# The modulation filler of the scans: loads of 2048 columns into one buffer in place of 512 into four

## The chip, the cores and the metric

The kernel runs on one core of one Trainium2 chip. The time is the device time of one execution in microseconds (us), the median of several runs. TensorE multiplies; VectorE (DVE), ScalarE (ACT) and GpSimd (POOL) work element by element; SyncE (SP) issues nearly all loads from DRAM.

## The reference, cut to what matters

Two blocks in a row work on 512 latent tokens and 256 context tokens of 1024 channels. The first block has two layers. Each layer's modulation is a product of a short vector with a large matrix, and it shifts, scales and gates everything else in the layer:

```python
silu_c, silu_cc = jax.nn.silu(c), jax.nn.silu(c_ctx)
for l in range(DEPTH):                                   # two layers
    mod_x = (silu_c @ ada_w[l] + ada_b[l])[:, None, :]   # ada_w[l]: 1024 x 6144
    mod_c = silu_cc @ ada_w[l] + ada_b[l]
    ...
    yc, s_f, s_b = rwkv_scans(prep_c, s_zero, s_zero, emit=not last)
    yx, _, _ = rwkv_scans(prep_x, s_f, s_b, emit=True)   # a recurrence over the tokens, both directions
    ...
```

The second block has a modulation of the same size (`w_ada`), attention and a mixture of experts. So there are three modulation matrices of 1024 x 6144, 24 MB each in float32. Each is read once and multiplied with two vectors only (latents and context): there is much to load and little to compute.

## The kernel before, in words

**The modulation.** `ada` (lines 365 to 390) works on groups of 2048 columns; three groups make a matrix, so there are nine. For each of the eight blocks of 128 rows (`k`) it loads pieces of `ada_w` columns (line 373, on SP's queue) into a buffer `wraw` from `raw()` (line 297), and multiplies each 512 columns (line 376): the stationary operand is `cs`, 128 x 32 with the two vectors in its first two columns, the moving operand 128 x 512 in float32. The four 512-column parts of a group go to four column groups of TensorE's array (`tile_position=(0, 32 * q)`) and to four sets of 32 partitions of one PSUM bank, which sums over the eight `k`. A profile shows each such matmul as two records. Afterwards ScalarE copies the bank (line 379) into a buffer `BF`, four transposes (line 382) turn the columns onto the partitions, and VectorE adds the bias.

**Where it runs.** The first group is done before the first layer. The other eight are filler in the scans: `scans` (line 1166) treats four head pairs a layer, and after each it emits `filler(hp)`, which is one group of 2048 columns. Four fall in layer 0's scan (about 365 to 830 us), four in layer 1's (about 1760 to 2215 us).

**The scan around it.** For each head pair `scan_in` prepares the operands (loads of `kr` and of `upr`), `scan_inv` inverts 32 x 32 blocks on VectorE (31 steps of two operations), `scan_x` and `scan_pre` make per-chunk matrices by many small products, loading `UV` on SP's queue, and `scan_run` is the recurrence itself: twelve chunks, at each a few 64 x 64 products on TensorE (lines 910 and 916) and one addition on VectorE that the next chunk's products need. A depthwise convolution (`conv_diag`, tile `cvp`) is spread between them. `BF` has one buffer: the filler's copy comes after the transposes (line 813) of its own head pair, and those of the next pair come after the filler's.

**What sets the order.** The program is built with `schedule_with_timeline_sim=True`: a planner places the instructions of each engine by priority and by its own estimate of the times, and every engine then runs its list strictly in order. Each head pair's filler is emitted with `high_priority(offset=1000)`, so it is placed as soon as its operands are there by that estimate, ahead of the scan's own work.

**The buffers.** `open_r` (line 2166) opens the pools of the scans. There `K.ada_w = 512` and `K.nw = 4`: each load is 128 x 512 (256 KB), and four buffers of 2 KB a partition rotate. A load waits for the matmul that last read its buffer. In the other stages `ada_w` is 1024; the first group, before layer 0, isn't touched.

Of the kernel before, what the change touches and what calls it, by code (L numbers as in the profile page):

```python
# [8 lines left out]
F32 = mybir.dt.float32  # L9
# [15 lines left out]
# ---------------------------------------------------------------- host layout  # L25
class Vecs:
    """Per-channel vectors side by side, channel on the partition."""
# [19 lines left out]
def pack_m(w):  # L47
    """[K, M] -> [M/128, 128, K/128 * 128]: the k-tiles of one column block side by side."""
    k, m = w.shape
    return np.ascontiguousarray(  # L50
        w.reshape(k // 128, 128, m // 128, 128).transpose(2, 1, 0, 3).reshape(m // 128, 128, -1))


def host(I):
# [26 lines left out]
    for l in range(2):  # L81
# [8 lines left out]
        up = np.stack([I["decay_up"][l], I["iclr_up"][l]], 0)               # [2, dir, 64, 512]  # L90
# [6 lines left out]
    qa = w[:, :512].reshape(1024, 2, 4, 64).transpose(0, 2, 1, 3).reshape(1024, 512)   # heads (j, 4 + j) side by side  # L97
# [63 lines left out]
def consts():  # L161
    """Depend on shapes alone."""
# [20 lines left out]
# ---------------------------------------------------------------- the kernel  # L183
# [4 lines left out]
class Stat:  # L188
    """sums of squares over the channels, a column per 128 tokens, from tiles as they come"""
# [24 lines left out]
class Kern:  # L214
    def __init__(self, tc, A, pvat, out, dbg=None):
        self.tw, self.narrow = NT, False
        self.tc, self.nc, self.A, self.at, self.out = tc, tc.nc, A, pvat, out
        self.dbg_out = dbg or {}
        self.V, self.S, self.G, self.T = tc.nc.vector, tc.nc.scalar, tc.nc.gpsimd, tc.nc.tensor
        self.moe_ps, self.queue, self.spare, self.wpre = False, None, [], []  # L220
        self.ada_w = 1024
        self.th = ""               # the strand of work that emits: buffers are handed out in order within each
        self.phm, self.ppm, self.psh = {}, {}, {}     # pools of a strand of its own

    # -- small helpers
# [39 lines left out]
    def rsqrt(self, t, n, name):  # L265
        """t[128, n] > 0 -> 1/sqrt(t), by bits and three Newton steps."""
# [15 lines left out]
    def pin(self, ins):  # L282
        """behind what its engine was given before"""
        return self.tc.keep_in_program_order(ins)
# [11 lines left out]
    # -- weights  # L296
# [18 lines left out]
    def dense(self, src, act, segs, done, kts=8, m=128):  # L315
        """out[m, tok] = w^T act in three passes of float32r; done(i, seg, psum)."""
# [14 lines left out]
    def flush(self, g, mid=None):  # L331
        """the products put off: the first g side by side, a term of each in turn; mid: emitted after their weights;
        what it returns: a step of it per term, done before the last"""
# [20 lines left out]
    # -- adaLN: columns of silu(c) @ w + b, both streams  # L354
# [10 lines left out]
    def ada(self, w, cs, bname, mod, groups, pth=None):  # L365
        """mod[128, 48, 2] += for the groups of 2048 columns."""
        for g in groups:
# [15 lines left out]
            # column q*128 + 32 j + s of tp: block 4 j + q of the group, stream s  # L383
# [8 lines left out]
    # -- rms norm and modulation, channel-major  # L392
    def modcols(self, mod, gname, sh, sc, name):
        """a = g (1 + sc), b = sh for both streams: [128, 8, 2]."""
# [5 lines left out]
    def normstat(self, tiles, segs, name):  # L400
        """1 / rms, on all partitions"""
# [18 lines left out]
    def spread(self, r, segs, name):  # L420
        """a column per 128 tokens as rows on all partitions"""
# [10 lines left out]
    def normmod(self, tiles, segs, a, b, name, streams=None, full=False, dst=None, bcs=None, ahead=False):  # L432
        """hi/lo of rms(x) a + b (full: itself, in dst where given)."""
# [43 lines left out]
    def normmod2(self, tiles, ms, g, a, b):  # L477
        """hi/lo of rms(xb) a + b with xb = rms(x) g, over the latents; then xb in x's place.
        rms(xb)'s mean square is that of x g over the mean square of x; ms: both."""
# [35 lines left out]
    # -- group norm over the 64-channel groups of a tile, tokens at the offsets of segs  # L515
    def gn_center(self, t, segs, name, pin=False):
        """t -= group mean (in place)."""
# [7 lines left out]
    def grp_rstd(self, sq, segs, scale, eps, name, floor=None, rb=None):  # L525
        """psum per seg: rsqrt(sum over the tile's two 64-channel groups * scale + eps)."""
# [23 lines left out]
    # -- token shift of width 3  # L550
# [13 lines left out]
    def wi_tile(self, l, mt, segs, name, out=None):  # L564
        """one column block of the RWKV part of u, shifted. mt counts blocks of 128 after the conv part.
        Where the product is put off, what shifts it."""
# [20 lines left out]
    # -- the scan of one head pair, both directions. Per chunk of 64 tokens:  # L587
    #    A, B (alpha with beta, kappa), D, E (rho with beta, kappa), X = (1 + A)^-1,
    #    U = -X (alpha S + B V), y = rho S + D U + E V, S' = f (S + beta U + kappa V);
    #    with W = X alpha and U0 = -X B V that is S' = M S + c, y = R S + y0 where  # L590
    #    M = f (1 - beta W), c = f (beta U0 + kappa V), R = rho - D W, y0 = D U0 + E V
    def units(self, d, q):
        """first chunk of the direction's batch q"""
        return (8, 0, 4)[q] if d == 0 else (8, 4, 0)[q]
# [5 lines left out]
    def scan_in(self, l, hp, kvs, kt=None, rt=None, kk=None):  # L600
# [9 lines left out]
        off = (self.ph if hp % 2 else ph).tile([128, 24, 32], F32, name="off", bufs=1)      # rows 0-31, 64-95: the block beside the diagonal  # L610
# [21 lines left out]
        for d in range(2):  # L632
# [15 lines left out]
            V.tensor_scalar(thw, thw, -0.5 * DEC, -0.5 * DEC, op0=ALU.mult, op1=ALU.add)   # log decay  # L648
# [28 lines left out]
            # kappa = Eb k (1 + (a - 1) ka), beta = Eb kk a, a = (1 + tha) / 2  # L677
# [11 lines left out]
            # A, for the reverse direction with alpha's token on the partition; its diagonal 32 x 32 blocks go to  # L689
            # lane 8 b + 4 s + i of quadrant (direction, half)  # L690
# [19 lines left out]
    def scan_inv(self, inv=None):  # L710
# [3 lines left out]
        # inverses of the 32 x 32 blocks, one block to a partition  # L714
# [19 lines left out]
    def scan_x(self, off, G1, G2):  # L734
        V, S, G, T = self.V, self.S, self.G, self.T
        # X transposed: diagonal blocks, and -(T2 A21 T1)^T (forward), -(T1 A12 T2)^T (reverse)
# [34 lines left out]
    def scan_pre(self, l, hp, H):  # L771
        """per chunk M and R (over alpha and rho), c and y0"""
# [8 lines left out]
        def early(q, d):  # L781
# [9 lines left out]
            # the two heads on two halves of the rows, side by side  # L791
# [16 lines left out]
            # f beta and f kappa with the token on the partition  # L808
# [10 lines left out]
            # f on the diagonal in alpha's place  # L819
# [69 lines left out]
    def scan_run(self, l, hp, H):  # L889
        """the recurrence over chunks, both directions in step"""  # L890
# [4 lines left out]
        for q in range(3):  # L895
            full = l == 0 or q > 0
            ub = [self.units(d, q) for d in range(2)]
            # the half of the batch with the smaller chunk numbers first
# [30 lines left out]
    def scan_out(self, l, hp, y, kvs, segs, out=None):  # L929
        """group norm, bonus and gate, in place; the last pair's into out"""  # L930
# [31 lines left out]
    def token_terms(self, l, hp, kt, vt, rt, kvs, segs):  # L962
        """normed removal key, bonus of the current token and gate, to DRAM"""
# [4 lines left out]
        # v with the token on the partition  # L968
# [38 lines left out]
    def conv_z(self, l, ci, segs):  # L1007
        """value * sigmoid(gate) (twice), zero-padded: x at 15, ctx at 557."""
# [26 lines left out]
    def conv_taps(self, l, ci, z, segs, pool):  # L1035
        """the depthwise convolution"""
# [20 lines left out]
    def conv_norm(self, l, ci, tiles, segs, mixd):  # L1057
        """twice the silu of the group norm"""
# [21 lines left out]
    def project(self, l, kvs, mixd, zd, lw):  # L1080
        """w_in and the token shift"""
# [9 lines left out]
        # high and low parts over each other: [hi; lo] of w, [lo; hi] of a  # L1091
# [41 lines left out]
    def conv_diag(self, l, ci, zd, segs, steps):  # L1133
        """the depthwise convolution as products with diagonals, in steps"""
# [76 lines left out]
    def mixer_out(self, l, kvs, mixd, mod, spill):  # L1211
        """x + gt1 (mix @ w_out)"""
# [53 lines left out]
    def ffn(self, l, xt, r2, a2, b2, mod):  # L1266
        """x + gt2 (swiglu), in place; the hidden columns in three parts."""
# [56 lines left out]
    # ------------------------------------------------------------ second block  # L1324
# [4 lines left out]
    def rope(self, t, out, name):  # L1329
        """t [128, 512] of the latents -> out"""  # L1330
# [8 lines left out]
    def head_norm(self, t, segs, g):  # L1339
        """rms over the 64 channels of each head, in place."""  # L1340
# [7 lines left out]
    def ctx_ahead(self, mod):  # L1348
        """the second block's normed context"""
# [8 lines left out]
    def qkv(self, xt, ms, mod):  # L1358
        """x (after the first block's norm), queries, keys and token-major values."""
# [25 lines left out]
        def piped(jobs):  # L1385
            """two products ahead of what follows one"""
# [21 lines left out]
        def lat(i):  # L1408
            def first():
# [4 lines left out]
                self.dense(self.A["wqkv"][i], hx, xs, done)    # 0-3 qa, 4 ka, 5-8 qb, 9-12 kb  # L1414
# [22 lines left out]
    def lambda_col(self):  # L1437
        """[128, 1]: minus lambda"""
# [17 lines left out]
    def split_q(self, q, first=False):  # L1456
        """times -1/8, per head, high parts on its own partitions and low parts on the others"""
# [10 lines left out]
    def split_k(self, k, first=False):  # L1468
        """per head, high parts on both halves of the partitions; low parts"""
# [10 lines left out]
    def softmax(self, q, k, s, qt):  # L1480
        """unnormalised exp of the scores of 128 queries and 1 / row sum; the queries carry -1/8, so that the
        scores' maximum is the least here"""
# [3 lines left out]
        sc = self.psc.tile([128, NT], F32, name="sc")       # starts on a bank or in its middle  # L1486
# [20 lines left out]
    def attention(self, mod):  # L1507
# [3 lines left out]
        steps = []           # (scores and exp, what follows) in order  # L1511
# [108 lines left out]
    def rows_ahead(self, mod):  # L1620
        """scale, shift and gate of the experts' norm as rows in DRAM; the router's part that all tokens share"""
        V, S, G, T, nc, A = self.V, self.S, self.G, self.T, self.nc, self.A
        # the sum of what the experts make of a token, zero at first
# [30 lines left out]
    def out_proj(self, mix, mod):  # L1654
        """Output projection and residual, token-major in Y; what the routing needs of it, as the tiles come:
        the mean squares, and the products with the router's weights before the norm's scale of a token."""
# [12 lines left out]
        # expert biases in two exact parts  # L1669
# [57 lines left out]
    # ------------------------------------------------------------ experts  # L1727
# [4 lines left out]
    def moe_route(self):  # L1732
        """Everything before the experts: normed rows, routing, slots."""
# [8 lines left out]
        # normed rows, token-major, in two exact parts  # L1742
# [707 lines left out]
```

## Time and profile before

Three runs took 4617.17, 4621.30 and 4623.69 us.

| | |
|---|---|
| median of the runs | 4621.3 us |
| span of the profiled execution, its first to its last instruction | 4622.1 us |
| TensorE (PE) busy | 4289.2 us, 93% of the span |
| VectorE (DVE) busy | 2919.9 us, 63% |
| ScalarE (ACT) busy | 2070.3 us, 45% |
| GpSimd (POOL) busy | 963.8 us, 21% |
| mean granted clock of TensorE, 1 is 2.4 GHz | 0.939 |
| loads of modulation weights in the scans | 256 of 256 KB, 2.9 us to land |

The profiled execution's own time is its span; the runs' median is 0.8 us below it. "Busy" is the time in which an engine has at least one instruction under way. Matmuls overlap, and several in different parts of the array count once. "PE" is a matmul, "PEld" the load of its stationary operand. L376 is line 376. An arrow `<-` stands between what is written and what is read, or, behind an idle time, ahead of what ended it. A row with `xN` merges N records.

### The profile page before, as it was taken

Reading aid. Unit: us, or ns where it says so; the run is one execution under the profiler, and the core shown is the slowest. Engines: PE = TensorE matmul, PEld = TensorE weight load, DVE = VectorE, ACT = ScalarE, POOL = GpSimd, SP = SyncE. Lnnn points to the kernel's source line nnn. Section 1 sums busy time; section 2 is a strip of 40 time slices with the busy share of each in tenths; the row PEclk is TensorE's granted clock in tenths of the full one; section 3 lists DMA queues with packets and bytes.
Section 4 is the critical chain, followed back from the end, with each engine's and each line's share of the span. In section 5 each row is a group of like instructions: output and inputs, shape, how many; then the busy total and the mean of one; then the engine's idle time right before and its main releaser. Section 6 shows DMA issues by size and latency. Waiting matters only on the chain.

```text
span 4622.1 us, 68704 instructions
## 1 busy us (share of the span) xinstructions
PE 4289.2 (93%) x26930; PEld 3276.4 (71%) x26930; DVE 2919.9 (63%) x4417; ACT 2070.3 (45%) x3140; POOL 963.8 (21%) x796
## 2 busy tenths in 40 slices
PE   7888999999999888899899999998899999999997
PEld 5664565888888664455788886666777777777775
DVE  6884675433333884755444355645888888888887
ACT  4554332231212553432323242343566666766665
POOL 1552121000000441111000032102323223323222
PEclk9888999999999998889999998798999999999998
DMA  4224323311112224322332241003799989999896
GB/s 157 69 90 128 103 88 107 106 60 64 64 61 80 69 86 134 92 88 84 116 105 92 87 146 41 3 1 126 239 306 305 309 300 303 306 309 304 306 303 244
DMA packets 249438, 691.04 MB, mean 150 GB/s; under 512 B 52055, under 2 KB 60912, under 8 KB 249106
## 3 DMA queue, kind: packets, MB, share of 16 engines
q1 hardware_dynamic: 224354, 636.25, 40.9%
q0 software_dynamic: 7808, 20.74, 1.9%
q10 hardware_dynamic: 16944, 29.58, 1.9%
q8 instruction: 214, 3.51, 0.3%
q14 instruction: 118, 0.97, 0.1%
HBM read 643.12 MB, written 51.45 MB: 150 GB/s over the span
## 4 chain that ended last, share of the span: by engine, by line
PE 42%; DMA 6%; DVE 3%; issue 1%; ACT 1%; POOL 0%; SPq 0%; DVEq 0%; POOLq 0%; ACTq 0%
DMA yd<-ye,ixs 5%; PE dps L326 4%; PE dps L328 4%; PE dps L327 4%; PE acc L1930 4%; PE acc L1931 4%; PE acc L1929 4%; PE acc L1953 3%; PE acc L1954 3%; PE acc L1952 3%; PE tok L1872 2%; PE sc L1489 2%; PE sc L1488 1%; PE av L1535 1%; PE tp L1503 1%; DVE elo L1911 1%
## 5 line engine op out<-in xcount | busy, mean ns | idle before, releaser
L1909 ACT CAST ehi<-eraw 128x1024 fp32r<-128x1024 f32 x768 | 803.1, 1051 | 381.4 <-PE acc L1931 229.3
L1911 DVE TENSOR_TENSOR elo<-eraw,ehi 128x1024 fp32r<-128x1024 f32 x640 | 865.3, 1390 | 97.7 <-ACT ehi L1909 95.5
L309 ACT CAST whi<-wraw 128x1024 fp32r<-128x1024 f32 (+1 forms) x234 | 239.5, 1028 | 768.1 <-PE dps L327 416.0
L1911 POOL TENSOR_TENSOR elo<-eraw,ehi 128x1024 fp32r<-128x1024 f32 x128 | 331.3, 2588 | 847.8 <-ACT ehi L1909 771.8
L310 DVE TENSOR_TENSOR wlo<-wraw,whi 128x1024 fp32r<-128x1024 f32 (+1 forms) x234 | 292.2, 1251 | 225.6 <-ACT whi L309 222.3
L1930 PE MATMUL acc<-elo,ex 128*128 128x512 f32 x1024 | 416.0, 406 | 14.4 <-DVE elo L1911 13.2
L1929 PE MATMUL acc<-ehi,ex 128*128 128x512 f32 x1024 | 408.7, 399 | 0.3 <-ACT ex L1875 0.3
L1931 PE MATMUL acc<-ehi,ex 128*128 128x512 f32 x1024 | 408.0, 398 | 0.0
L327 PE MATMUL dps<-h2l,whi 128*128 128x512 f32 x992 | 351.2, 354 | 0.0
L326 PE MATMUL dps<-h2h,whi 128*128 128x512 f32 x992 | 351.1, 354 | 0.0
L328 PE MATMUL dps<-h2h,wlo 128*128 128x512 f32 x992 | 350.3, 353 | 0.0
L1930 PEld LDWEIGHTS acc<-elo,ex 128*128 128x128 f32 x1024 | 194.7, 190 | 65.4 <-DVE elo L1911 20.6
L376 PE MATMUL adaps<-wraw,cs 128*32 128x512 f32 x576 | 234.6, 630 | 2.8 <-DMA wraw<-in_ada_dram 1.8
L1929 PEld LDWEIGHTS acc<-ehi,ex 128*128 128x128 f32 x1024 | 194.7, 190 | 47.3 <-issue 0.7
L328 PE MATMUL dps<-hh,wlo 128*128 128x512 f32 (+3 forms) x568 | 209.5, 370 | 17.6 <-DVE wlo L310 17.6
L1931 PEld LDWEIGHTS acc<-ehi,ex 128*128 128x128 f32 x1024 | 194.6, 190 | 39.3
L326 PE MATMUL dps<-hh,whi 128*128 128x512 f32 (+3 forms) x568 | 210.4, 370 | 5.5 <-ACT whi L309 4.9
L1953 PE MATMUL acc<-elo,eah 128*128 128x512 f32 x512 | 206.9, 404 | 1.7 <-DVE elo L1911 1.7
L326 PEld LDWEIGHTS dps<-h2h,whi 128*128 128x128 f32 x992 | 188.0, 190 | 26.4
L327 PE MATMUL dps<-hl,whi 128*128 128x512 f32 (+3 forms) x568 | 206.8, 364 | 0.0
L1952 PE MATMUL acc<-ehi,eah 128*128 128x512 f32 x512 | 203.5, 397 | 3.3 <-DVE ye L1972 3.3
L328 PEld LDWEIGHTS dps<-h2h,wlo 128*128 128x128 f32 x992 | 187.8, 189 | 26.1
(605 smaller groups left out, 9508.8 us busy)
## 6 DMA issues: line engine op xcount, KB each, us to landing
eraw<-in_ewi_dram SPq DMA_DIRECT2D x503, 512.0 KB, 6.0
eraw<-in_ewo_dram SPq DMA_DIRECT2D x256, 512.0 KB, 5.2
wraw<-in_ada_dram SPq DMA_DIRECT2D x256, 256.0 KB, 2.9
wraw<-in_wi_dram SPq DMA_DIRECT2D x44, 512.0 KB, 3.8
wraw<-in_wg_dram SPq DMA_DIRECT2D x44, 512.0 KB, 3.7
wraw<-in_wu_dram SPq DMA_DIRECT2D x44, 512.0 KB, 3.7
wraw<-in_wd_dram SPq DMA_DIRECT2D x32, 512.0 KB, 3.7
wraw<-in_wqkv_dram SPq DMA_DIRECT2D x28, 512.0 KB, 3.7
```

The lines of the kernel that those rows point to most:

```text
L309: self.S.copy(hi, raw)
L310: i = self.V.tensor_tensor(lo, raw, hi.bitcast(F32), ALU.subtract)
L326: self.T.matmul(ps, w0, h[:, o:o + n], start=k == 0, stop=False)
L327: self.T.matmul(ps, w0, l[:, o:o + n], start=False, stop=False)
L328: self.T.matmul(ps, w1, h[:, o:o + n], start=False, stop=k == kts - 1)
L1909: self.S.copy(hi, raw)
L1911: (self.G if self.wn % 6 == 0 else self.V).tensor_tensor(lo, raw, hi.bitcast(F32), ALU.subtract)
L1929: T.matmul(acc[:, N], xh[:, K], wh[:, W], start=False, stop=False)
L1930: T.matmul(acc[:, N], xh[:, K], wl[:, W], start=False, stop=False)
L1931: T.matmul(acc[:, N], xl[:, K], wh[:, W], start=False, stop=k == 7)
L1952: T.matmul(acc[:, N], ah[:, K], wh[:, N], start=k == 0, stop=False)
L1953: T.matmul(acc[:, N], ah[:, K], wl[:, N], start=False, stop=False)
```

## The change

Two values in `open_r` differ. In the scans a load is now 128 x 2048 (1 MB, 8 KB a partition) and there is one buffer `wraw`; its size is that of the four together. In `ada` the loop over `hf` then has one step in place of four, and its inner loop over `j` four in place of one: the same 256 matmuls, 32 a group, read the same columns in the same order from 64 loads.

```diff
 def open_r(K, ph):
     ...
     K.n3.update(c=3, v=1, f=1), K.np.update(e=1, b=3, c=1, f=1)
-    K.ada_w, K.tw, K.nhl = 512, NT, 2
-    K.nw, K.nuv, K.nkd = 4, 3, 3
+    K.ada_w, K.tw, K.nhl = 2048, NT, 2
+    K.nw, K.nuv, K.nkd = 1, 3, 3
```

The loop that they act on, which is the same in both:

```python
for k in range(8):
    for hf in range(2048 // self.ada_w):
        raw = self.raw()[:, :self.ada_w]
        o = g * 2048 + hf * self.ada_w
        self.nc.sync.dma_start(raw, w[k * 128:(k + 1) * 128, o:o + self.ada_w])
        for j in range(self.ada_w // 512):
            q = self.ada_w // 512 * hf + j
            self.T.matmul(ps[32 * q:32 * q + 32, :], cs[:, k, :], raw[:, j * 512:(j + 1) * 512],
                          start=k == 0, stop=k == 7, tile_position=(0, 32 * q))
```

The rest of the diff takes out comments and docstrings.

## Rows read from the trace of the kernel before

**Rows 1.** The page: span, and busy time of TensorE.

```profile
span 4622.1 us, 68704 instructions
PE 4289.2 (93%) x26930; PEld 3276.4 (71%) x26930; DVE 2919.9 (63%) x4417; ACT 2070.3 (45%) x3140; POOL 963.8 (21%) x796
```

**Rows 2.** Busy by stretch: from:to, us, PE PEld DVE ACT POOL, clock, DMA share, GB/s.

```profile
365.00:427.00 62.00, 59.11 (x554) 24.39 (x556) 21.68 (x44) 24.78 (x57) 9.43 (x14) 0.85 0.58 165
427.00:490.00 63.00, 55.78 (x646) 38.91 (x646) 53.63 (x123) 22.80 (x56) 12.79 (x21) 0.89 0.16 45
490.00:546.00 56.00, 55.29 (x627) 25.79 (x622) 27.83 (x64) 20.87 (x52) 7.77 (x12) 1.00 0.48 147
546.00:602.00 56.00, 53.58 (x700) 40.86 (x695) 49.65 (x124) 29.05 (x72) 16.52 (x22) 0.94 0.21 65
602.00:665.00 63.00, 62.92 (x775) 32.60 (x774) 42.48 (x98) 23.86 (x57) 10.59 (x16) 1.00 0.44 132
665.00:706.00 41.00, 39.09 (x541) 29.40 (x540) 34.77 (x93) 12.99 (x31) 13.52 (x18) 1.00 0.17 52
706.00:765.00 59.00, 59.00 (x629) 26.90 (x628) 22.32 (x51) 11.03 (x23) 5.85 (x11) 1.00 0.46 139
1760.00:1822.00 62.00, 60.19 (x554) 25.75 (x554) 17.20 (x35) 25.02 (x58) 6.92 (x11) 0.89 0.55 167
1822.00:1858.00 36.00, 34.34 (x455) 25.25 (x453) 26.69 (x60) 18.00 (x46) 6.55 (x10) 0.91 0.19 53
1858.00:1913.00 55.00, 55.00 (x522) 26.69 (x520) 35.45 (x89) 15.48 (x41) 8.23 (x11) 1.00 0.51 152
1913.00:2006.00 93.00, 63.91 (x758) 45.94 (x759) 75.94 (x188) 39.04 (x97) 12.07 (x17) 0.65 0.12 33
2006.00:2066.00 60.00, 60.00 (x681) 28.26 (x676) 21.48 (x48) 19.98 (x48) 5.30 (x9) 1.00 0.49 144
2066.00:2117.00 51.00, 44.82 (x567) 33.15 (x565) 46.09 (x116) 14.29 (x30) 11.92 (x15) 0.80 0.11 29
2117.00:2176.00 59.00, 59.00 (x637) 28.01 (x637) 14.72 (x38) 11.40 (x24) 5.54 (x8) 1.00 0.45 138
```

**Rows 3.** The same of the filler's matmuls alone, eight stretches: their sum.

```profile
sum 476.00, PE 223.92 PEld 29.01; mean PE 27.99 PEld 3.63
```

**Rows 4.** Timeline of TensorE: start, us, engine, line, tiles, form, records.

```profile
489.82 1.07 PE L376 MATMUL adaps<-wraw,cs 128*32 128x512 f32 x8
490.81 1.09 PE L846 MATMUL mrp<-KD,UV 64*64 64x128 f32 x16
...
496.30 1.05 PE L376 MATMUL adaps<-wraw,cs 128*32 128x512 f32 x2
497.28 0.70 PE L1159 MATMUL cvp<-z,cvd 128*128 128x256 f32 x2
```

**Rows 5.** DMA issues: tiles, queue, count, KB each, median us to landing.

```profile
wraw<-in_ada_dram SPq DMA_DIRECT2D x256, 256.0 KB, 2.9
wraw<-in_wg_dram SPq DMA_DIRECT2D x44, 512.0 KB, 3.7
```

**Rows 6.** Last group: first burst, copy of its sums, and what such copies wait for.

```profile
2117.56 0.64 PE L376 MATMUL adaps<-wraw,cs 128*32 128x512 f32 x4
...
2201.61 0.58 ACT L379 COPY BF<-adaps 128x512 f32<-128x512 f32 x1 [2.03 <-PE tp L813]
...
  PE tp L813: 25.8, 6
```

**Rows 7.** The filler's matmuls from 365 to 2215 us: idle TensorE before them.

```profile
  DMA wraw<-in_ada_dram: 3.3, 7
```

**Rows 8.** Timeline: four loads are issued on SP, and TensorE's first use of them.

```profile
707.10 1.77 SPq L373 DMA_DIRECT2D wraw<-in_ada_dram  x4
...
711.88 1.05 PE L376 MATMUL adaps<-wraw,cs 128*32 128x512 f32 x4
```

**Rows 9.** DMA issues from 365 to 400 us, the first scan's start.

```profile
kr<-kvs SPq DMA_DIRECT2D x3, 384.0 KB, 7.9
```

## The prediction

> **What bounds the kernel now.** I read the page's first part and then the busy time of each engine stretch by stretch. The page says that TensorE is busy for 4289 of 4622 us [rows 1], but that is an average, and the change touches only the two scans (365 to 830 us and 1760 to 2215 us). So the second view cuts these into the eight stretches in which a filler group runs (476 us) and the six stretches between them (340 us) [rows 2]. The reader is to compare the two kinds. With a filler group TensorE is busy for 470.5 of 476 us (the sum of eight rows), VectorE for 203 us (43%), at a mean granted clock of 0.966 (weighted by length; each moment is at 2.4 GHz, which is 1, or at 1.2). Without one TensorE is busy for 291.5 of 340 us (86%), VectorE for 287 us (84%), clock 0.834. So the filler stretches wait for TensorE and little else; between them the two engines wait for each other.
>
> The third view is the filler's own share of this: its 256 matmuls (512 records, two passes each) hold TensorE for 223.9 us of the 476 [rows 3]. The fourth shows why so much. At 489.82 the four matmuls of one row, in four column groups of the array, start together: eight records in 1.07 us, and the next product starts 0.99 us after the first. At 496.30 one matmul alone takes 1.05 us, and the next product starts 0.98 us after it [rows 4]. Four side by side cost what one costs. The kernel before pays the cheap price for the first row of each group, whose four loads are long there, and then places most matmuls singly, because each waits for a load of its own.
>
> **What is removed.** Four matmuls of a row now wait for one load and become ready together. 64 rows at 1.06 us are 68 us in place of 223.9: TensorE loses 156 us of issue time. (A few of the rows now run at half clock, in the first group of each scan [rows 2]; a burst there costs about 2 us, some 8 us over all groups, which I leave inside the range.) The Trainium skill weighs on this term: "TensorE: Matmul & The Clock Gate", Part 3, says of column tiles that three of them give a speedup of 2.38, not 3; by that ratio (0.79) four would cost 1.26 singles, and the term would be 138 us instead of 156. The 0.99 us of the burst against 0.98 us of the single shows no such loss, so the trace decides for 156.
>
> SP issues 64 loads in the scans in place of 256, at 0.33 us or more each, and has a quarter as many waits for a free buffer. It isn't the bound, so this is worth nothing by itself. The bytes are the same, and so is the buffer's size (8 KB a partition).
>
> **What is added.** (a) With one buffer, row r+1 can't be loaded before row r is multiplied. A load of 1 MB isn't in this trace. From below: it can't be quicker than the 3.7 us of 512 KB; from above: four of 256 KB one after another, 4 x 2.9 = 11.6 us [rows 5]. I take the line through the two rows, 3.7 + 2 x 0.8 = 5.3 us (an estimate from them). A row then cycles in 1.06 + 5.3 = 6.4 us, and a group of eight in about 46 us (at 11.6 us: 90 us). What has to come of it is the copy out of the filler's bank, and this copy waits for TensorE's transposes of the scan, not for the filler: in the last group the first burst stands at 2117.56 and the copy at 2201.61, 84 us later [rows 6]. Even a stretch shortened by 20 us leaves 64 us for a chain of 46, so its length costs nothing, and at 11.6 us a load it would cost some 26 us a group. (b) TensorE runs in order. If a row's four matmuls stand in its queue before their load has landed, the whole scan behind them waits: the products of the recurrence and whatever VectorE needs of them. In this trace the filler's loads held TensorE for 3.3 us in the scans, 7 times [rows 7]; a load issued at 707.10 is used at 711.88, 4.8 us later, though 256 KB land in 2.9 us [rows 5, 8]. The order, which is made from an estimate of the times, thus leaves about 2 us to spare, and for a four times larger load I expect it to keep some of it. From below this costs nothing; from above, if a row's matmuls stand where those of a 256 KB load would, 5.3 - 2.9 = 2.4 us on each of 56 rows, 134 us. I take 5 us, near the row of 3.3, all of it at the start of the first scan, where the loads of kr take 7.9 us to land [rows 9]. (c) On SP's queue the scan's own loads (kr, UV, z, gb) stand behind a load that waits for its buffer. They did so before, in front of loads with the same total; a UV load may find 1 MB ahead of it and come a few us later, which its three buffers cover. Without them it would be a few us once per batch, 48 times.
>
> **The sum.** If TensorE alone set the eight stretches, 156 us would go. But VectorE and the recurrence take over where TensorE steps back. The stretches without a filler show how tightly the two then run. TensorE's remaining 314.6 us (470.5 less 156) at their busy share of 0.857 take 367 us in place of 476: a gain of 109. If the clock also falls from 0.966 to their 0.834, the same work takes 425 us: a gain of 51. Bursts every few us keep TensorE fuller than in those stretches, but the order will also push some bursts into them, so I take the middle of these two, 80, and take off the 5 us of (b): 75 us. The profile's own time of 4622.1 us is within 0.8 us of the median of the runs, 4621.3, so nothing has to be carried over: 4622 - 75 = 4547 us. This likeliest case, 4500 to 4590, has a chance of 0.6.
>
> **The rivals.** First, the whole gain: VectorE is 43% busy in the filler stretches and could follow, the rows spread into the stretches that now have idle TensorE, and the clock stays up. Gain 110 to 156, 4465 to 4512 us. For it: 203 us of VectorE in 476. Against it: the 0.834 of the clock wherever TensorE isn't full. Chance 0.17.
>
> Second, slower: the load takes the place of the matmuls. Each row's burst stands at the head of TensorE's queue and waits out its load. The price is the upper end of (b): 56 x 2.4 = 134 us against the 75 to 80 gained, so some 4676 us; it decides from 80 / 56 = 1.4 us of waiting a row. For it: with one buffer nothing is ever loaded ahead within a group, and TensorE with less to do between bursts gets back to the next one sooner. Against it: the spare 2 us and the short waits of [rows 7, 8], and that TensorE has about 250 us of other work in the filler stretches, 4 us or so for each row, besides what it has between them. The Trainium skill speaks for this rival: "Trainium Kernel Development and Optimization", Best Practices, asks for double buffering so that transfers lie beside compute, and the change gives that up; no run so far shows what it costs here. Chance 0.13.
>
> Third, nothing: the recurrence (twelve chunks a head pair, TensorE and VectorE in turn) sets each stretch, and the saved slots turn into idle TensorE at a lower clock. 4612 to 4625 us. Against it: TensorE is idle for at most 3 us in each of the eight stretches, VectorE for 57% of their time. Chance 0.05. Fourth, the four matmuls don't stand together, since work that is more urgent comes between them; then, with pairs and threes lost again, perhaps a quarter of the 156 us goes, 39, and at the rate of the main case (75 of 156) the gain is 10 to 30 us, 4592 to 4612. Against it: where four loads were there, as at 489.82, the four were taken together. Chance 0.05.
>
> **How the numbers follow.** The range reaches from inside the first rival to the small gains, 4480 to 4606 us; outside it lie most of the slower rival and the best third of the first, together under 0.2. A change of 0.2%, 9 us, is what a measurement of this kernel can just tell from none. Faster by more than that: 0.6 + 0.17 + most of the fourth rival = 0.82; the same 0.05; slower 0.13.
>
> **What would show it.** In the profile after: 64 loads of 1024 KB on the modulation weights in the scans, landing in about 5.3 us; the filler's matmuls in bursts of eight records, TensorE's time on them 65 to 80 us in place of 223.9; the two scans (465 and 455 us before) each some 35 to 40 us shorter; TensorE's busy share in the filler stretches down from 99% to about 85%, with a clock below 0.966. After the scans nothing should move but the offset. I am wrong if TensorE waits for the filler's loads by more than 1.4 us a row, if the bursts are broken up, or if the two scans keep their length while TensorE's idle time grows by what the filler gave up.

## The result, and the profile after

Four runs of the changed kernel took 4514.1 to 4528.4 us, median 4519.9; four of the kernel before 4617.2 to 4623.7, median 4620.9. The ratio is 0.9782, 95% interval 0.9767 to 0.9797: 101 us faster. The page after, answering [rows 1] and [rows 5]:

```profile
span 4516.9 us, 68323 instructions
PE 4167.7 (92%) x26930; PEld 3267.0 (72%) x26930; DVE 2919.0 (65%) x4417; ACT 2069.4 (46%) x3140; POOL 970.9 (21%) x796
...
wraw<-in_ada_dram SPq DMA_DIRECT2D x64, 1024.0 KB, 5.0
```

TensorE is busy 121 us less, the span is 105 us shorter, and the other engines do what they did. The 1 MB load lands in 5.0 us (5.3 forecast).

Where the time went is read in two windows, each from a scan's first product on tile `m` to its last on `yp`. Columns are those of [rows 2]. First the kernel before:

```profile
370.90:821.50 450.60, 433.80 (x5323) 260.23 (x5322) 281.64 (x674) 163.81 (x380) 87.98 (x125) 0.96 0.37 110
1763.10:2220.20 457.10, 415.91 (x4877) 246.23 (x4876) 262.65 (x635) 158.73 (x367) 67.75 (x97) 0.88 0.35 106
sum 907.70, PE 849.72 PEld 506.46 DVE 544.29 ACT 322.55 POOL 155.73; mean PE 424.86 PEld 253.23 DVE 272.14 ACT 161.27 POOL 77.87
...
sum 907.70, PE 221.36 PEld 28.81; mean PE 110.68 PEld 14.40
```

The last line is the sum for the filler's matmuls alone. The same of the kernel after:

```profile
372.10:796.30 424.20, 386.75 (x5322) 266.37 (x5322) 279.75 (x674) 163.46 (x380) 87.06 (x125) 0.88 0.36 117
1734.50:2126.70 392.20, 351.10 (x4875) 240.03 (x4876) 265.99 (x635) 157.24 (x366) 72.84 (x97) 0.85 0.38 122
sum 816.40, PE 737.85 PEld 506.39 DVE 545.75 ACT 320.70 POOL 159.89; mean PE 368.93 PEld 253.20 DVE 272.87 ACT 160.35 POOL 79.95
...
sum 816.40, PE 87.78 PEld 11.40; mean PE 43.89 PEld 5.70
```

This gives an account that every kernel below gets too: a scan's time is TensorE's time on the filler, its time on everything else, and its idle time. Filler 221.4 to 87.8 (-133.6); everything else 849.7 - 221.4 = 628.4 to 650.1 (+21.7); idle 907.7 - 849.7 = 58.0 to 78.5 (+20.5). Together -91.3 us: 26 in layer 0's scan, 65 in layer 1's.

"Everything else" needs care: a product that runs beside a filler matmul is counted as filler. By the trace's single records 28.2 us of other products did so before and 7.8 do so after, so that by themselves the other products take 656.5 us before and 657.9 after. About 20 of the 21.7 us are a matter of counting. What the clock costs (0.88 and 0.85 for 0.96 and 0.88) shows if each moment in which TensorE is busy is weighted with the clock granted in it: that is 790 us of work at full clock before and 634 after, 156 less. The busy time fell by only 112 us, so some 45 us came back through the clock, and 20 more as idle time. The other 14 us of the span lie outside the scans, 12 of them after the second. All fourteen kernels timed here run the same code behind the scans and take between 2386 and 2412 us for it (2402 before, 2390 after), so I don't put these 12 us down to the change.

The filler stretches themselves, first to last burst of a group, answering [rows 2], and the stretches between and behind them; each part ends with the sum over its eight:

```profile
365.00:428.00 63.00, 56.03 (x723) 35.03 (x724) 35.16 (x74) 33.13 (x76) 13.10 (x18) 0.78 0.55 167
459.00:520.00 61.00, 50.24 (x654) 29.62 (x652) 50.16 (x118) 25.38 (x67) 12.22 (x18) 0.85 0.45 152
...
1732.00:1797.00 65.00, 60.11 (x699) 37.28 (x699) 33.46 (x69) 31.92 (x74) 10.68 (x15) 0.71 0.52 168
...
sum 481.00, PE 429.86 PEld 265.97 DVE 298.01 ACT 199.03 POOL 82.58; mean PE 53.73 PEld 33.25 DVE 37.25 ACT 24.88 POOL 10.32
...
1880.00:1933.00 53.00, 46.13 (x521) 33.53 (x519) 43.09 (x109) 21.01 (x54) 10.65 (x13) 0.79 0.15 44
...
sum 344.00, PE 313.48 PEld 241.23 DVE 252.72 ACT 124.72 POOL 80.46; mean PE 39.19 PEld 30.15 DVE 31.59 ACT 15.59 POOL 10.06
```

The eight filler stretches did not get shorter: 481 us for 476. In them VectorE now works 298 us in place of 203, and TensorE does more of the scan's own work. What shrank is the rest of the two scans: 822 - 365 + 2214 - 1760 - 476 = 435 us before, 344 after. So the freed slots are filled with scan work that used to come after the group.

Timeline of TensorE after, answering [rows 4]:

```profile
695.44 1.07 PE L376 MATMUL adaps<-wraw,cs 128*32 128x512 f32 x8
696.43 0.27 PE L856 MATMUL cyp<-KD,UV 128*64 128x64 f32 x1
...
702.67 1.07 PE L376 MATMUL adaps<-wraw,cs 128*32 128x512 f32 x8 [1.19 <-DMA wraw<-in_ada_dram]
703.67 1.09 PE L846 MATMUL mrp<-KD,UV 64*64 64x128 f32 x16
...
709.85 1.06 PE L376 MATMUL adaps<-wraw,cs 128*32 128x512 f32 x8
```

And of SP in the same 15 us:

```profile
696.56 0.34 SPq L373 DMA_DIRECT2D wraw<-in_ada_dram  x1
...
703.80 0.33 SPq L373 DMA_DIRECT2D wraw<-in_ada_dram  x1
```

A row is eight records in 1.07 us, and the next product starts 0.99 us after the first. The next load is issued right behind the burst (696.56, 703.80) and the next burst stands 7.2 us after the last. One of the two gaps ends in a wait for the load, 1.19 us. Over both scans, idle TensorE ahead of the filler's matmuls, then which of its instructions waited for the loads, answering [rows 7]:

```profile
  DMA wraw<-in_ada_dram: 57.3, 46
  issue: 8.5, 23
...
  PEld adaps L376: 31.6, 24
  PE adaps L376: 25.7, 22
DMA to landing us min/median/max: 4.7/4.9/9.6
```

Before, the first line read 3.3 us in 7 [rows 7]. But it adds up two lists: the idle time ahead of loading the stationary operand (PEld, during which earlier products may still run) and the idle time ahead of the matmul (PE). By the single records nearly every microsecond of the second lies inside the first, so that a wait is counted twice. The products themselves stand still for 25.7 us, in 22 waits; before it was 1.1 us in 2. That is the number to set beside the 78.5 us of idle time above. The copy of the sums still waits for the scan's transposes, as in [rows 6]:

```profile
  PE tp L813: 15.3, 6
```

### The profile page after: what moved, and what is told of

Same layout as the page of the kernel before. It is cut to its first block, busy times and chain, and to the rows that moved or that the text cites. A ratio compares the mean times of both kernels' runs of the same rounds, so it can differ in the third digit from the quotient of the medians.

```text
span 4516.9 us, 68323 instructions
## 1 busy us (share of the span) xinstructions
PE 4167.7 (92%) x26930; PEld 3267.0 (72%) x26930; DVE 2919.0 (65%) x4417; ACT 2069.4 (46%) x3140; POOL 970.9 (21%) x796
## 4 chain that ended last, share of the span: by engine, by line
PE 49%; DVE 8%; DMA 7%; issue 2%; ACT 1%; POOL 0%; SPq 0%; ACTq 0%; DVEq 0%; POOLq 0%
DMA yd<-ye,ixs 5%; PE dps L326 4%; PE dps L327 4%; PE dps L328 4%; PE acc L1930 4%; PE acc L1929 4%; PE acc L1931 4%; PE acc L1953 3%; PE acc L1954 3%; PE acc L1952 3%; PE tok L1872 2%; PE sc L1489 1%; PE sc L1488 1%; PE av L1535 1%; PE tp L1503 1%
## 5 line engine op out<-in xcount | busy, mean ns | idle before, releaser
L327 PEld LDWEIGHTS dps<-h2l,whi 128*128 128x128 f32 x992 | 188.2, 190 | 25.8
```

Source lines behind the costliest of these rows:

```text
L327: self.T.matmul(ps, w0, l[:, o:o + n], start=False, stop=False)
```

## The experiments

Theory at the start (A): the gain comes of TensorE's slots, four matmuls side by side behind one load; how many loads bring a row, and with how many buffers, hardly matters. Rivals: the fewer loads do it (B); the waits for the single buffer eat a good part (C); the planner happened on a better order (D). Each kernel's account of its two scans, worked out as above (its two windows, its filler sum, the difference to the windows' length), with the two scans' granted clock and the median of its runs. An account is of one profiled execution; the runs of the changed kernel differ by 14 us, so a difference of some 10 us between two accounts can be scatter:

| kernel | scans | filler | else | idle | clock | median us | ratio, 95% |
|---|---|---|---|---|---|---|---|
| before | 907.7 | 221.4 | 628.4 | 58.0 | 0.96, 0.88 | 4620.9 | |
| after | 816.4 | 87.8 | 650.1 | 78.5 | 0.88, 0.85 | 4519.9 | 0.977-0.980 |
| two1024 | 844.3 | 140.0 | 638.9 | 65.3 | 0.92, 0.87 | 4561.7 | 0.986-0.991 |
| halfrow | 849.0 | 96.6 | 664.6 | 87.8 | 0.86, 0.86 | 4593.3 | 0.993-0.997 |
| split_cols | 920.4 | 222.9 | 643.6 | 53.9 | 0.91, 0.90 | 4623.6 | 0.998-1.001 |
| split_rows | 907.0 | 94.5 | 696.1 | 116.4 | 0.80, 0.78 | 4627.3 | 1.000-1.002 |
| after_short | 804.9 | 83.2 | 643.6 | 78.2 | 0.88, 0.86 | 4531.1 | 0.979-0.984 |
| before_bf16 | 881.3 | 103.0 | 716.2 | 62.1 | 0.83, 0.75 | 4590.7 | 0.992-0.996 |
| after_bf16 | 817.6 | 32.0 | 702.0 | 83.5 | 0.83, 0.74 | 4509.8 | 0.972-0.977 |
| no_filler | 762.7 | 0 | 690.3 | 72.4 | 0.83, 0.76 | 4465.8 | 0.962-0.968 |
| before_pri500 | 877.5 | 175.7 | 638.3 | 63.5 | 0.90, 0.88 | 4584.7 | 0.989-0.993 |
| after_pri500 | 801.0 | 94.1 | 637.7 | 69.1 | 0.90, 0.86 | 4531.2 | 0.978-0.983 |
| before_pri1400 | 925.9 | 228.8 | 645.1 | 52.0 | 0.90, 0.91 | 4627.9 | 1.000-1.003 |
| after_pri1400 | 837.9 | 84.1 | 666.7 | 87.1 | 0.84, 0.82 | 4547.1 | 0.981-0.987 |

**Two buffers of 1024 columns (two1024).**

```diff
-    K.ada_w, K.tw, K.nhl = 2048, NT, 2
-    K.nw, K.nuv, K.nkd = 1, 3, 3
+    K.ada_w, K.tw, K.nhl = 1024, NT, 2
+    K.nw, K.nuv, K.nkd = 2, 3, 3
```

> In the scans the filler loads 1024 columns into two buffers (128 loads of 512 KB; the same 8 KB a partition). Theory T (TensorE's time on single matmuls was the price, side by side gives it back, what is left of the price is waiting for loads): pairs side by side make 128 slots of about 1.05 us, 134 us on TensorE in place of 224 before and 91 after, and with a second buffer the waits for loads fall from 57 us to under 20: about 4550 us, between before (4621) and after (4520). Rival L (fewer and larger loads are what helps, by freeing SP's queue for the scan's own loads): half of the gain or more, 4540 to 4570, and the same time as the run with half rows, whose loads are as many and as large. Rival O (the planner happened on a better order): no relation to the slots, anything from 4520 to 4621.

Measured 4561.7 us, 59 of the 101. The matmuls stand in pairs (103 of 124 bursts) and the filler holds TensorE for 140 us, between 221 and 88. The scans are 63 us shorter than before; a filler shorter by 81 went into it. So a burst half as wide brought a bit more than half of the gain. The expected fall of the waits failed to come: by the list with both entries 43 us are left of 57, on the matmuls alone 16.7 of 25.7.

**Four side by side, 256 columns of each part, two buffers (halfrow).**

```diff
+    ...                                        # src: the row's weights, seen as four parts of 512 columns
+    self.nc.sync.dma_start(raw.rearrange("p (q c) -> p q c", q=4), src[:, :, hf * 256:hf * 256 + 256])
+    for q in range(4):
+        self.T.matmul(ps[32 * q:32 * q + 32, hf * 256:hf * 256 + 256], cs[:, k, :], raw[:, q * 256:(q + 1) * 256], ...)
```

> 128 loads of 512 KB into two buffers as in the run with 1024 columns, but each holds 256 columns of all four column groups, so that four matmuls of 256 columns stand side by side for each load. T: TensorE's time on the filler is 65 to 80 us, the waits for loads under 20 us, since the next half is loaded while this one is multiplied: 4480 to 4505 us, faster than after and by 40 us or more faster than two loads of 1024. L: the same time as the run with 1024 columns within 10 us. O: no relation.

Missed: 4593.3 us (4570 to 4607; the profiled execution had 4568). The filler falls to 96.6 us as thought, but a second buffer takes no wait away: its matmuls stand still 32 times for 26 us until a load lands (22 times and 25.7 us in the changed kernel), and idle and everything else are 9 and 15 us above the changed kernel's. The profiled execution is the fastest of six, so the account shows too little of the loss. Each of its 128 loads is one more place to wait at, and each reads runs of 1 KB; which of the two weighs more no run separates. It is the first sign against "how many loads hardly matters". Against B stands that two1024 has the same 128 loads of the same size and is 32 us quicker, though its runs are 4 KB long. (Two buffers of 2048 columns were not tried.)

**The row in four loads, by columns and by partitions (split_cols, split_rows).** In both one buffer of 2048 columns, filled by four loads of 256 KB. By columns each matmul waits for its own quarter again; by partitions each needs all four quarters, so that the four become ready together.

```diff
+    ...                                        # j runs over the four loads
+    self.nc.sync.dma_start(raw[:, j * m:(j + 1) * m], w[k * 128:(k + 1) * 128, o + j * m:o + j * m + m])   # split_cols, m = 512
+    self.nc.sync.dma_start(raw[p:p + m], w[k * 128 + p:k * 128 + p + m, o:o + self.ada_w])                 # split_rows, m = 32
```

> The kernel after with its one buffer, but each row comes in four loads of 512 columns, and each matmul needs only its own. T2: the matmuls fall apart into singles, pairs and threes again, TensorE's time on the filler rises from 91 us to 140 to 220, and the time goes back to 4570 to 4640 us: the difference to the run with loads split by rows is the grouping alone, 40 us or more. L: 4595 to 4625, like the run split by rows. O: no relation to either.

> The kernel after, but each row of 2048 columns comes in four loads of 32 partitions (256 KB each, 256 loads as before), so that each matmul still needs all four and they still become ready together. Theory T2 (four matmuls side by side free TensorE; the clock, which falls where TensorE has less to do, takes part of it back; the number of loads is incidental): some 90 us of TensorE on the filler, and the time of after plus the issue of three more loads a row, at most 1.2 us on 56 rows: 4515 to 4570 us. Rival L (fewer and larger loads, a free SP queue): back to 4595 to 4625, with loads as many and as small as before. Rival O (the planner's order by chance): anything from 4520 to 4620.

split_cols: 4623.6 us, no gain, and the filler is back at 222.9 us. Without the burst the single large buffer gives nothing. split_rows: 4627.3 us, no gain either, though the burst is there (62 of 64 rows whole) and the filler takes 94.5 us. That was a miss, and it is the more telling kernel. Its two scans, what the filler's matmuls and their weight loads waited for (us, times, longest), and the DMA queue of SP in its second scan (packets, MB, share of 16 engines):

```profile
371.80:841.50 469.70, 411.36 (x5321) 281.81 (x5322) 276.75 (x674) 164.09 (x380) 85.62 (x125) 0.80 0.43 105
1781.00:2218.30 437.30, 379.29 (x4875) 256.41 (x4876) 264.32 (x635) 159.25 (x367) 70.90 (x97) 0.78 0.46 111
...
PEld adaps L379 <- issue: 85.9, 45, 6.7
PE adaps L379 <- DMA wraw<-in_ada_dram: 77.3, 35, 6.6
...
q1 hardware_dynamic: 22764, 44.81, 43.8%
```

The same queue in the second scan of the changed kernel:

```profile
q1 hardware_dynamic: 21108, 44.50, 34.7%
```

For the same bytes within 1% the DMA engines are busy 0.438 x 437 = 191 us in place of 0.347 x 392 = 136; in split_cols, with as many loads, but each over all partitions, it is 139. Rows follow each other at 9.0 us in place of 7.6 (median spacing of first matmuls within the groups). The filler's products stand still for 77.3 us until a load lands, 1.2 us a row, against 25.7 and 0.4 in the changed kernel; the PEld line mostly shows the same waits from the side of the weight load. Idle grows by 38 us and everything else by 46, at a clock of 0.80 and 0.78: with the filler's 7 the 91 us are gone. So A falls in its second half: the burst is needed, and it pays only if the row comes quickly, here in one load over all partitions. This is the prediction's second rival, in part: the row's wait is there, and the lower clock takes as much again.

Both kernels came out where B had them (4595 to 4625 us), split_rows 2 us above. B's mechanism is not in the traces, though: in the kernel before, the engines wait for the scan's own loads on SP's queue (kr, upr, UV, z, gb) for 2.7 us in all, as the line below shows, and with fewer filler loads these land hardly sooner (medians before and after: UV 2.9 and 2.9 us, kr of 384 KB 5.1 and 4.8, gb of 384 KB 3.0 and 5.1). What 64 large loads would give without the burst no run shows.

```profile
ACT uph L625 <- DMA upr<-in_up_dram: 2.7, 4, 1.1
```

**A quarter of the bytes (after_short).**

```diff
+    n = 512 if self.th == "f" else self.ada_w
+    self.nc.sync.dma_start(raw[:, :n], w[k * 128:(k + 1) * 128, o:o + n])
```

> The kernel after, but each row loads only its first 512 columns (256 KB; the other three quarters of the weights are left out, and the four matmuls read the same 512). T: loads land in about 2.9 us in place of 5.0, TensorE's waits for them fall from 57 us to under 15, and since a group's chain of loads is what its stretch waits for, the time falls to 4475 to 4500. If the waits are hidden (what follows them would have waited anyway): 4510 to 4525.

Its account, and its matmuls' wait for loads:

```profile
sum 804.90, PE 726.74 PEld 500.16 DVE 541.26 ACT 322.50 POOL 156.03; mean PE 363.37 PEld 250.08 DVE 270.63 ACT 161.25 POOL 78.02
...
  DMA wraw<-in_ada_dram: 6.8, 9
```

Missed: 4531.1 us, no faster than the changed kernel. The matmuls' waits for loads fell from 25.7 to 6.8 us (57.3 to 16.3 by the list with both entries), but TensorE's idle time stayed (78.2 for 78.5): other waits took their place. The scans are 11.5 us shorter, hardly more than scatter. So against C, taking away three quarters of the waits for the single buffer buys some 12 us, if anything.

**Half the passes (before_bf16, after_bf16).** The matmuls of either kernel read the upper halves of the same numbers, in one pass.

```diff
+    ... cs[:, k, :].bitcast(BF16)[:, 1::2], raw.bitcast(BF16)[:, 1024 * j + 1:1024 * (j + 1):2] ...
```

> The kernel before, 512 columns into four buffers, but the filler's matmuls in the scans read only the upper halves of the numbers, as bf16 (the modulation is less exact), so that a single matmul takes one pass and not four. T: some 0.3 us a slot, 60 to 90 us on TensorE in place of 224, no more waits than before: 4500 to 4530 us, though not one load differs. L: 4610 to 4625, since loads and SP's queue are those of before. O: 4590 to 4640.

> The changed kernel with the scans' filler matmuls done in one pass over bf16 halves of the same buffers (the modulation vectors come out rounded): the same 64 loads, half the TensorE passes. Theory (the clock gives back what TensorE is relieved of, as in before_bf16): filler time falls from 91 us to 45 to 65, the granted clock in the scans falls below 0.875 and 0.852, and the time stays at 4495 to 4530 us. Rival (TensorE's time on the filler is still what sets the scans, and the clock follows only when TensorE waits): 30 to 45 us less, 4475 to 4490 us, clock as in the changed kernel.

Scans of before_bf16, and its filler:

```profile
370.60:817.60 447.00, 416.26 (x5199) 285.80 (x5198) 285.75 (x674) 164.20 (x381) 85.09 (x125) 0.83 0.36 111
1757.00:2191.30 434.30, 402.89 (x4751) 277.28 (x4752) 262.90 (x635) 158.40 (x367) 71.03 (x97) 0.75 0.37 112
...
sum 881.30, PE 102.97 PEld 19.99; mean PE 51.49 PEld 9.99
```

The same of after_bf16:

```profile
370.70:784.90 414.20, 372.38 (x5199) 272.31 (x5198) 283.77 (x674) 165.15 (x381) 86.09 (x125) 0.83 0.37 119
1726.10:2129.50 403.40, 361.71 (x4751) 266.07 (x4752) 264.23 (x635) 158.47 (x367) 75.28 (x97) 0.74 0.37 121
...
sum 817.60, PE 32.04 PEld 8.07; mean PE 16.02 PEld 4.04
```

before_bf16 was a miss: its filler shrinks by 118 us, nearly as much as by the change, but the scans only by 26. Everything else takes 716 us in place of 628 at 0.83 and 0.75; 0.75 means half the time at 2.4 GHz and half at 1.2. (28 us of other products run beside the filler in either, so here the difference is not one of counting.) after_bf16 came out as the theory had it in time and clock, with even less filler than thought: 56 us less filler, 52 us more of everything else, scans 816 to 818. So TensorE's time on the filler is not the whole story: the same number of microseconds taken off by a shorter matmul is given back by the clock, and taken off by four matmuls side by side most of it is kept. At about equal filler time (88 and 103 us) the clock is 0.88 and 0.85 with four float32 matmuls side by side and 0.83 and 0.75 with single bf16 ones. It isn't the width that makes the difference: after_bf16 has bursts and 0.83 and 0.74, and without any filler it is 0.83 and 0.76 (below). The bf16 filler thus keeps the clock no higher than none, the float32 filler of the changed kernel does; why, no run here shows.

**No filler (no_filler).** The eight groups are left out, and the modulation they would compute is zero.

```diff
-            with pri(1000):
-                filler(hp)
```

> The kernel after without the filler of the scans: neither its loads nor its matmuls nor the copies run, and the modulation that it would make is zero. T2: the scans lose 91 us of TensorE's time and 57 us of waits, but the clock falls below the 0.86 of after, so that less than 60 us of it is seen: 4460 to 4510 us. If the filler of after is already all but hidden: 4505 to 4525, with the scans as long as after's 816 us. If TensorE's time and the waits all count: 4370 to 4420.

4465.8 us; scans 762.7, of which everything else is 690.3 at 0.83 and 0.76. The filler's price in the scans was thus 145 us before, for 221 us of slots, and is 54 now, for 88. Without it everything else takes 62 us more than before, though the copies and transposes of the filler are gone too: 28 us because no product runs beside a filler matmul any more, the other 34 at the lower clock. TensorE idles 14 us more. So a third of the filler's 221 us cost nothing, for these three reasons.

**The order (before and after at priority offsets 500 and 1400 in place of 1000).**

```diff
-            with pri(1000):
+            with pri(500):      # in the other two, 1400
                 filler(hp)
```

> The kernel after with the filler's priority raised by 500 places in place of 1000, which gives the planner another order for the same work. T2: bursts of four still, some 90 us of TensorE on the filler: 4500 to 4550 us. O: the gain was a lucky order, and another one loses it: 4560 to 4620.

> The kernel before (loads of 512 columns, four buffers) with the filler emitted at priority offset 500 in place of 1000, as in after_pri500. Theory (the gain of the change comes of four matmuls side by side behind one load, not of the order that the planner happens to make): the loads are as they were, so most filler matmuls stand alone, TensorE's filler time stays at 200 to 240 us and the time at 4600 to 4640 us. Rival (a later filler alone makes a better order): filler time about the same, but scans shorter by 40 us or more, 4540 to 4580 us.

> The changed kernel with the filler emitted at priority offset 1400 in place of 1000. Theory (the gain doesn't hang on one order): filler time 85 to 110 us, waits for the loads 40 to 80 us, 4500 to 4545 us. Rival (offset 1000 happens to suit one buffer, and an earlier filler makes TensorE wait out each load): waits of 100 us or more, 4560 to 4620 us.

> The kernel before with the filler at priority offset 1400: the third pair of before and after at one offset (500: 4585 and 4531; 1000: 4621 and 4520 us). Theory (the loads' form gives about 50 to 100 us at any offset, the order that the planner finds moves either kernel by some 20 to 40 us more): filler time 215 to 240 us, 4600 to 4645 us, that is 50 to 100 above the 4547 us of the changed kernel at this offset. Rival (the order gives most of the gain, and offset 1000 was merely a bad order for the kernel before): 4550 to 4590 us, under 45 us above it.

At 500 the gain of the change is 4584.7 - 4531.2 = 54 us, at 1000 101, at 1400 81; in the scans 77, 91 and 88. So the change helps at every offset, by 54 to 101 us, and D holds for a part: the kernel before gets some 40 us shorter by a later filler alone (ratio 0.991), which neither expectation had (4600 to 4640, or 4540 to 4580). The account names its source, the filler's sum over 365 to 2230 us (224.4 in the same window of the kernel before):

```profile
sum 1865.00, PE 175.68 PEld 23.29; mean PE 175.68 PEld 23.29
```

Placed later, its matmuls hold TensorE for 176 us instead of 224, by the order alone, still with 256 loads (which again is against B). More of them stand side by side: in its trace they form 147 bursts, 89 of a single matmul, in place of 206 and 174. The reason is likely that they find more of their loads landed. after_pri1400 was just outside its range (4500 to 4545). No variant of the changed kernel that computes the full result was faster than the changed kernel itself.

## Why the prediction was right

**TensorE's slots.** The step was right and its size too large: 156 us forecast, 134 measured, and 88 us on the filler where 65 to 80 had been named as the sign. The bursts are there at the rate of the single matmul (60 of 64 rows whole). The shortfall is mostly the clock, which I had set at 8 us over all groups. A burst in the second scan, from the chain that ended last, and the same 2 us by stretch, with a clock of 0.50:

```profile
1752.97 1.92 PE adaps L376 x8
...
1752.90:1754.90 2.00, 2.00 (x12) 0.28 (x12) 2.00 (x7) 0.59 (x1) 0.00 (x0) 0.50 0.03 8
```

At full clock a burst takes 1.05 to 1.07 us; 18 of the 71 bursts took longer, nearly all of these 1.93. That is some 16 of the 20 us that lie between 68 and 88. The Trainium skill's ratio for column tiles ("TensorE: Matmul & The Clock Gate", Part 3) would have given 138, an estimate near the 134. But at full clock four side by side still cost 1.07 us, so the trace doesn't agree with the ratio, and the shortfall has another reason.

**The wait for the loads.** The load was sized well (5.0 us for 5.3), the row's cycle slightly short (7.6 us for 6.4, since TensorE takes the burst up some time after the landing). The step that failed is (b): 5 us taken, 25.7 measured on the matmuls, 0.4 us a row, within its bounds of 0 and 134. (The 3.3 us that I put beside it were counted twice, as above; on the matmuls they were 1.1.) The 2 us to spare were misread, too. For the four loads issued from 707.10 us I took the median landing of 2.9 us, but where the profile tells the landing of one of these four, it took

```profile
DMA to landing us min/median/max: 4.1/4.3/4.5
```

so of the 4.8 us up to the first use perhaps half a microsecond was spare. The old order left little cover, and none for a load of 5.0 us. By after_short the waits cost little, some 12 us for three quarters of them. The second rival's turning point, 1.4 us of waiting on each of 56 rows, was near the mark: split_rows waits 77.3 us, which over 56 rows is 1.4, and comes out even. Its working was not: I took all the loss as waiting, and there idle time grows by only 38 of the 91 us.

**What is given back.** I took 80 of 156 us as kept (a busy share and a clock of the stretches without filler); 91 of 134 were kept in the scans, even with the waits inside. Weighted with the clock it is 91 of 156: 45 came back through the clock and 20 as idle time. The clock fell as foreseen, to 0.86 in the filler stretches (weighted by length) from 0.966, with TensorE busy for 89% of them (85 forecast). What I had wrong is the place: the filler stretches didn't shrink at all; the stretches behind them did, since their work was pulled forward into the slots. The scans' shares, 26 and 65 us where I had 35 to 40 each, are probably a matter of order: in the kernel before the second scan had a poor 93 us at a clock of 0.65 [rows 2], and the order at offset 500 alone takes 33 us out of it (457 to 424).

**The sum.** The profiled span is 30 us below the working's 4547: 16 us of that in the scans, 14 outside, where I expected nothing and where kernels with the same code scatter by 27 us. The likeliest case (4500 to 4590) came in. In the scans the forecast was 75 us and the measurement 91, from two errors of opposite sign: 22 us too much taken off TensorE, 39 us too much given back. That the sum came so near is in part luck.

**The rivals.** The whole gain (110 to 156) didn't come: 42 us of 134 were kept back, by the clock and by idle time. The slower one is real but needs a slower row than one 1 MB load gives; the Trainium skill's advice on double buffering ("Trainium Kernel Development and Optimization", Best Practices), which spoke for it, doesn't decide here: one buffer of 2048 columns beats two of 1024 by 42 us. "Nothing" and "bursts broken up" didn't occur; what broken bursts would have cost is seen in split_cols.

## What to carry to other kernels

If small matmuls of different column groups each wait for a load of their own, let one load over all partitions bring all of them: side by side they cost one slot, and here this was worth more than a second buffer. Count a saving on TensorE at less than its length wherever TensorE is the bound only on average: here a third came back, and with a shorter matmul (bf16) three quarters and more. And before a wait is added up from a list of idle times, see which unit each entry belongs to: one wait for a load can stand there twice, ahead of the weight load and ahead of the matmul. Last, take one more order of the same program before a difference of 1% is put down to an edit.

## What was not expected of the hardware

- Four loads over 32 partitions each keep the DMA engines 40% longer busy than one over 128 for the same bytes (191 us in split_rows for 136 in the changed kernel, second scan), while four loads over 128 partitions each do not (139 in split_cols). Each lands in 4.8 us, where 256 KB over 128 partitions took 2.9 in the kernel before and 3.8 in split_cols.
- The granted clock fell here when TensorE was given less to do: with the filler's matmuls cut from 221 to 103 us by bf16, everything else in the scans took 716 us (0.83, 0.75) in place of 628 (0.96, 0.88).
